# Output projection of a hybrid decoder block: sixteen plain products or one seven-product step

## The chip, the core and the metric

One core of one Trainium2 chip runs the whole program in one launch. Its engines work side by side, each through its own list of instructions in a fixed order, and wait for one another through semaphores: TensorE (PE in the profile) multiplies, VectorE (DVE), ScalarE (ACT) and GpSimd (POOL) work elementwise, and SyncE (SP) issues the transfers between DRAM and the on-chip memory SBUF. Products are written to PSUM, in eight banks of 128 x 512 float32. The metric is device time in microseconds (us), the median of the timed runs.

## The reference, cut to what matters

The program computes one decoder layer on 1024 tokens of width 1024, all in float32: a norm, an input projection, two groups of heads (retention and differential attention), the output projection with the residual, a second norm, and a SwiGLU feed-forward of width 2816.

```python
ret = ret * jax.nn.silu(rg)                       # [1, 1024, 512]
dif = (rms_norm(dif, diff_subln_g[l]) * (1.0 - LAMBDA_INIT)).reshape(B, S, DIFF_WIDTH)
mix = jnp.concatenate([ret, dif.astype(ret.dtype)], axis=-1)
x = x + jnp.einsum('bse,ed->bsd', mix, w_out[l]).astype(x.dtype)   # w_out 1024 x 1024
h2 = rms_norm(x, norm2_g[l])
ff = jax.nn.silu(jnp.einsum('bsd,df->bsf', h2, w_gate[l])) * jnp.einsum('bsd,df->bsf', h2, w_up[l])
x = x + jnp.einsum('bsf,fd->bsd', ff, w_down[l]).astype(x.dtype)
```

The change concerns the line with `w_out` and what stands next to it in time.

## The kernel before, in words

**Precision.** Every float32 operand of a product is split in two pages, `hi` (rounded to the matmul's fp32r type, a copy on ACT) and `lo` (the rest, a subtraction on DVE). One product of 128 x 128 by 128 x 512 is then three matmuls, hi·hi, hi·lo and lo·hi (`mm3`); I call that a triple.

**Stages.** Input projection of the attention heads and the attention itself run until about 225 us; the retention columns of the input projection follow, already as seven-product Strassen steps (`P1` to `P7`, one step for each half `p` of the retention heads), until about 420 us; then the output projection until about 541 us; then gate and up of the feed-forward, again as seven-product steps, until about 964 us; then the down projection, also in seven products.

**The output projection** (`o_proj`) takes sixteen pairs of a 128-token tile `t` and a column half `dh`, each with eight triples over the 1024 features: 16 x 8 x 3 = 384 matmuls. Its two operands are prepared beside it. `wo_prepare` loads a 128 x 512 page of `w_out`, scales and splits it (ACT and DVE). `mix_turn` loads the attention half of a token tile, transposes it and the retention half on PE, and splits both. When a pair is done, DVE adds the residual page of `x` from SBUF to the PSUM bank and SP stores the sum.

**What else runs in this stage.** The second four of the eight retention chunks of each half (`unit(p, t)`), a chain of small matmuls and DVE, ACT and POOL steps, are mixed in between the triples; `norm(t)` scales the finished rows and transposes them for the feed-forward; `f_sum` and `early_sums` form the sums of norm pages that the feed-forward's Strassen step needs as operands (`blk` names the seven operand pages). The first two feed-forward blocks' products (`first_product`) close this list.

**What sets the order.** Everything up to those first feed-forward products is registered with `add(engine, duration, ...)` in a list, and `Plan.times` works out an order for each engine: a list scheduling backwards from due times and forwards by assumed durations, tried with `SEEDS` small random shifts of the due times, the shortest kept. The order is then emitted as it stands, and the engines keep it. All those instructions are recorded by one helper, so the profile gives them all line L101, and groups are told apart by tiles: `h`, `pp`, `m` and `big` are PSUM banks, `whi`/`wlo` the split pages of the left operands, `sx` split pages of the right ones, `raw`, `pr`, `rowa` and `spare` plain pages, `wx`/`wy` the working pages of the retention chunks, `small` their row statistics. All plain transfers go through SP's one queue, in its order. The later feed-forward blocks are ordered by a hand-written pipeline (`class Strassen`), whose weight sums run on POOL (`sum<-rawp`, `sum<-wide`).

Of the kernel before, what the change touches and what calls it, by code (L numbers as in the profile page):

```python
# [72 lines left out]
def block_kernel(ctx: ExitStack, tc: tile.TileContext, x, norm1_g, w_in, ret_norm_g, dq_g, dk_g,  # L73
# [1057 lines left out]

    def wo_prepare(dh, k):
        key, page = wraw() if dh == 0 else wo1raw()
        dma(page, w_out[0, k * P:(k + 1) * P, dh * 512:(dh + 1) * 512], (), [key])
        hi, lo = wo_part(dh, k)
        kh, kl = wo_key(dh, k)
        scale = gout[:, min(k, 4):min(k, 4) + 1]
        after = [wo_after[dh][k // 4]]
        act_copy(hi, page, [key, "opened"], [kh], scale, after=after)
        stt(lo, page, scale, hi.bitcast(F32), ALU.mult, ALU.subtract, [key, kh], [kl], after=after)  # L1140
# [6 lines left out]
    xr_r = Ring(rawk)
    x2k = {}
    mT = {}

    DUE1 = {4: ("o", 0, 1), 5: ("o", 1, 1), 6: ("o", 1, 1), 7: ("o", 1, 1)}

    def mix_unit(t):
        if t < 4:
            key, page = prk[4 + t % 4]
            dma(page[:, 0:256], mixrd[t], [f"mixrd{t}"], [key])
        else:
            unit(0, t, marks[DUE1[t]])
        unit(1, t, marks[DUE1[t]] if t >= 4 else None)

    def mix_turn(t):
        key, page = px[t][1]
        dma(page, mixdd[t], [f"mixdd{t}"], [key])
        for q, (key, page) in enumerate((prk[4 + t % 4], px[t][1])):
            b = side_bank()

            def go(b=b, page=page):
                for j in range(4):
                    T.transpose(bank[b][:, j * P:(j + 1) * P], page[:, j * P:(j + 1) * P], ident)
            add("PE", 0.45, go, [key], [f"b{b}"])  # L1170
            n = 2 * (t % 2) + q
            hi, lo = slot[n]
            act_copy(hi, bank[b], [f"b{b}"], [f"wh{n}"], dur=0.48)
            tt(lo, bank[b], hi.bitcast(F32), ALU.subtract, [f"b{b}", f"wh{n}"], [f"wl{n}"])
# [417 lines left out]
```

## Time and profile before

| | value |
|---|---|
| median of three runs | 1179.95 us (1179.64, 1181.64, 1179.95) |
| the profiled execution | 1179.49 us |
| its span in the profile | 1177.7 us |
| PE busy | 1169.5 us, 99% of the span |
| DVE, ACT, POOL busy | 895.4, 604.5, 506.5 us (76%, 51%, 43%) |
| POOL between 419.95 and 545 us | 23.1 us, 44 instructions |

The span lies 1.8 us inside the execution's time. A share of busy time is a mean over stages that differ: POOL is at 43% over the whole program, but in the output projection it is nearly idle. Rows of a timeline give start, duration, engine, line, operation and tiles; rows of groups give busy time and the mean of one instruction after the bar, then the idle time ahead of the group's instructions with what ended most of it.

### The profile page before, as it was taken

How to read it: one execution, taken by the hardware profiler on the slowest of the kernel's cores; microseconds unless marked ns; L12 is line 12 of the kernel's file. 1: busy time of each engine (PE TensorE's matmuls, PEld its weight loads, DVE VectorE, ACT ScalarE, POOL GpSimd, SP SyncE). 2: the span in 40 equal slices, each digit the busy share in tenths (PEclk: the TensorE clock that was granted, in tenths of full speed). 3: DMA queues.
4: the chain of work that ended last, by engine and by line, in shares of the span. 5: the costliest groups of instructions: out<-in, count | busy, mean ns of one | idle time of the engine just before them, and what ended most of it. 6: DMA issues, size and time to landing. Idle time of an engine off the chain costs nothing.

```text
span 1177.7 us, 17427 instructions
## 1 busy us (share of the span) xinstructions
PE 1169.5 (99%) x5872; PEld 1004.7 (85%) x5872; DVE 895.4 (76%) x1561; ACT 604.5 (51%) x1332; POOL 506.5 (43%) x581
## 2 busy tenths in 40 slices
PE   9999999999999999999999999999999999999998
PEld 7999999988888888888888888888888888888887
DVE  6988888888779866758987756666665769698696
ACT  7767566666366745836444343434344334344442
POOL 4668786510012111301276654565456535263153
PEclk9999999999999999999999999999999999999999
DMA  7278776537644862322133423332323388933341
GB/s 213 69 173 150 136 115 117 162 124 235 223 126 148 266 201 90 95 88 90 58 131 117 134 76 98 111 119 90 99 99 116 106 293 265 354 101 90 98 138 67
DMA packets 118009, 164.29 MB, mean 139 GB/s; under 512 B 11936, under 2 KB 62240, under 8 KB 117792
## 3 DMA queue, kind: packets, MB, share of 16 engines
q1 hardware_dynamic: 110976, 152.62, 39.4%
q0 software_dynamic: 5760, 10.49, 6.5%
q8 instruction: 46, 0.75, 0.3%
q14 instruction: 43, 0.35, 0.1%
q10 hardware_dynamic: 1184, 0.07, 0.1%
HBM read 110.97 MB, written 54.26 MB: 140 GB/s over the span
## 4 chain that ended last, share of the span: by engine, by line
PE 93%; DVE 4%; ACT 2%; issue 1%; DMA 1%; SPq 0%; POOL 0%; DVEq 0%; ACTq 0%
PE h L101 39%; PE pp L101 31%; PE m L101 19%; PE big L101 4%; ACT pr L101 1%; DVE wx L101 1%; DVE wy L101 1%; DVE wlo L101 1%; DMA spare<-in_w_in_dram 1%; DVE pr L101 0%; DVE rowa L101 0%; DVE sx L101 0%; ACT wy L101 0%; DVE acc L101 0%; ACT whi L101 0%
## 5 line engine op out<-in xcount | busy, mean ns | idle before, releaser
L101 POOL TENSOR_TENSOR sum<-rawp 128x512 f32<-128x512 f32 x100 | 141.8, 1419 | 175.0 <-DVE wlo L101 144.9
L101 ACT CAST whi<-sum 128x512 fp32r<-128x512 f32 x155 | 96.4, 622 | 197.8 <-PE h L101 58.7
L101 DVE TENSOR_TENSOR wlo<-sum,whi 128x512 fp32r<-128x512 f32 x155 | 158.6, 1024 | 34.4 <-ACT whi L101 34.2
L101 PE MATMUL pp<-whi,act 128*128 128x384 f32 (+1 forms) x592 | 180.9, 359 | 0.2 <-DVE qkn L101 0.2
L101 POOL TENSOR_TENSOR sum<-wide 128x512 f32<-128x512 f32 x55 | 85.7, 1560 | 128.5 <-DVE wlo L101 101.8
L101 PEld LDWEIGHTS pp<-whi,act 128*128 128x128 f32 x592 | 109.4, 188 | 4.9 <-ACT q L101 0.6
L101 PE MATMUL h<-sx,whi 128*128 128x512 f32 x360 | 111.3, 390 | 0.0
L101 DVE TENSOR_TENSOR wlo<-wide,whi 128x512 fp32r<-128x512 f32 x99 | 77.5, 805 | 33.2 <-ACT whi L101 33.2
L101 ACT CAST whi<-wide 128x512 fp32r<-128x512 f32 x99 | 59.3, 621 | 84.2 <-PE m L101 43.3
L101 PE MATMUL pp<-wlo,act 128*128 128x384 f32 (+1 forms) x296 | 102.5, 346 | 0.0
L101 PEld LDWEIGHTS h<-sx,whi 128*128 128x128 f32 x360 | 67.2, 188 | 13.7
L101 DVE TENSOR_TENSOR wlo<-rawp,whi 128x512 fp32r<-128x512 f32 x44 | 48.6, 1105 | 38.6 <-ACT whi L101 37.7
L101 PE MATMUL h<-whi 128*128 128x512 f32 x196 | 76.7, 391 | 0.0
L101 DVE TENSOR_TENSOR c<-c,h 128x512 f32<-128x512 f32 x80 | 52.9, 681 | 31.3 <-PE h L101 31.3
L101 PE MATMUL h<-whi,wlo 128*128 128x512 f32 x196 | 76.3, 389 | 0.0
L101 PE MATMUL h<-wlo,whi 128*128 128x512 f32 x196 | 76.3, 389 | 0.0
L101 POOL TENSOR_TENSOR fsum<-c 128x512 f32<-128x512 f32 x50 | 70.7, 1426 | 8.1 <-DMA ffd<-fsum 8.1
L101 PE MATMUL h<-sx,wlo 128*128 128x512 f32 x180 | 70.1, 389 | 0.0
L101 POOL TENSOR_TENSOR stt<-stt,cs 128x1 f32<-128x1 f32 (+1 forms) x64 | 57.9, 906 | 3.7
L101 PEld LDWEIGHTS pp<-wlo,act 128*128 128x128 f32 x296 | 55.9, 189 | 1.9
L101 DVE CUSTOM_DVE_ANT_0 big<-big,zm 128x128 f32<-128x128 f32 (+7 forms) x64 | 47.7, 771 | 8.8 <-PE big L101 8.6
L101 PE MATMUL h<-b,whi 128*128 128x512 f32 x176 | 54.3, 390 | 0.0
(328 smaller groups left out, 3136.4 us busy)
## 6 DMA issues: line engine op xcount, KB each, us to landing
wide<-ffd SPq DMA_DIRECT2D x77, 256.0 KB, 2.7
ffd<-fsum SPq DMA_DIRECT2D x55, 256.0 KB, 2.0
rawp<-in_w_gate_dram SPq DMA_DIRECT2D x22, 512.0 KB, 3.5
rawp<-in_w_up_dram SPq DMA_DIRECT2D x22, 512.0 KB, 3.6
wide<-in_w_down_dram SPq DMA_DIRECT2D x44, 256.0 KB, 5.4
sumd<-act POOLq DMA_DIRECT2D x40, 256.0 KB, 4.2
rowa<-cd SPq DMA_DIRECT2D x32, 256.0 KB, 2.9
cd<-pr SPq DMA_DIRECT2D x24, 256.0 KB, 2.8
```

Of the source, the lines that this page charges most:

```text
L101: i = getattr(self.engine, op)(*(now(a) for a in args), **{k: now(a) for k, a in kw.items()})
```

## The change

The sixteen plain pairs are replaced by one Strassen step. Tokens, features and columns are halved; with A the mixed heads (columns: retention, attention) and B the output weights, seven products of a 512 x 512 block by a 512 x 512 block are formed, each in four token tiles of four triples: 7 x 4 x 4 x 3 = 336 matmuls.

- **Right operands** (`b_load`, `b_prepare`): 20 page loads in place of 16 (one quadrant's four pages are loaded twice, for products 3 and 6), each scaled in place by ACT. Five of the seven products need a sum or difference of two quadrants (20 pages, on POOL). All 28 operand pages are split, `hi` on ACT and `lo` on POOL. They go to two pages in turn (`HOME`).
- **Left operands** (`dif_turn`, `ret_turn`, `a_split`): the transposed tiles are copied to plain pages by ACT, DVE forms 20 sums and differences of quadrants, and 28 pages are split, `hi` on ACT, `lo` on DVE.
- **Results** (`o_product`, `o_add`): the residual pages are loaded ahead, and DVE adds each product to one or two of them, 40 additions in place of 16. Products 7 and 6 accumulate on the banks of 4 and 2 without clearing them.
- **Order**: products 4, 7, 1, 3, 5, then 2 and 6, which need the last retention chunks.
- **The feed-forward's first operands**: operand 3's sum and split and the nine `early_sums` go from DVE to POOL.
- **Homes**: new pages `kb` and `pg` (eight of 128 x 512 each) stand where `wo` and later operand pages stood; five of the seven `blk` pages get other homes; the cos/sin inputs of the later retention chunks come to pages of `rawp`. The planner tries 40 shifts, shifts only jobs from number 1700 on, and assumes 3.2 us of lag for a transfer in place of 2.8.

```diff
-                    j.shift = 0.0 if seed == 0 else 2.0 * (1 + seed % 3) * (...)
+                    j.shift = 0.0 if seed == 0 or j.n < SAME else 2.0 * (1 + seed % 3) * (...)
...
-    wo_block = [[sxt[0], sxt[2]], [None, lazy("wo")]]
...
+    HOME = {4: 0, 7: 1, 1: 0, 3: 1, 5: 0, 2: 1, 6: 0}
+    home_after = [[marks["P5", 3]], [marks["P7", 3]]]
...
+    def b_load(key, page, j, dh, k):
+        dma(page, w_out[0, (4 * j + k) * P:(4 * j + k + 1) * P, dh * 512:(dh + 1) * 512], (), [key])
+        act_copy(page, page, [key, "gout"], [key], gd if j else gout[:, k:k + 1])
+
+    TT_POOL = 1.5
+
+    def b_prepare(n, k):
+        (k0, b00), (k1, b11), (k2, b10) = kept_b[k], kept_b[4 + k], rowk[4 + k]
...
+        elif n == 1:
+            key, page = tmp_r()
+            tt(page, b00, b11, ALU.add, [k0, k1], [key], "POOL", TT_POOL)
...
+        hi, lo = b_part(n, k)
+        kh, kl = b_key(n, k)
+        act_copy(hi, page, [key], [kh], after=home_after[HOME[n]])
+        tt(lo, page, hi.bitcast(F32), ALU.subtract, [key, kh], [kl], "POOL", TT_POOL, after=home_after[HOME[n]])
...
+    def a_split(n, i, key, page, eng="DVE", dur=0.61):
+        at = A_SLOT[n] + i
+        hi, lo = slot[at]
+        act_copy(hi, page, [key], [f"wh{at}"])
+        tt(lo, page, hi.bitcast(F32), ALU.subtract, [key, f"wh{at}"], [f"wl{at}"], eng, dur)
...
+    def o_product(n, i, b, first=True):
...
+                for s_, (l, r) in enumerate(((ah, wh), (ah, wl), (al, wh))):
+                    T.matmul(bank[b], l[:, col], r, start=first and k == s_ == 0, stop=k == 3 and s_ == 2,
+                             skip_group_check=not first)
+            marks["o", n, i] = add("PE", MM3, go, [f"wh{at}", f"wl{at}"] + b_key(n, k), [f"b{b}"], main=True)
+
+    def o_add(t, dh, b, op=ALU.add):
+        key, page = px[t][dh]
+        tt(page, page, bank[b], op, [key, f"b{b}"], [key])
...
-    def o_proj(t, dh):
-        b = main_bank()
-        for k in range(KC):
...
-                mm3(bank[b], mh[:, col], ml[:, col], wh, wl, k == 0, k == KC - 1)
...
-        tt(page, bank[b], xr, ALU.add, [f"b{b}", xk], [key])
...
-    blk = [sxt[1], lazy("b1"), sxt[2], lazy("b3"), hT[1][1], sxt[0], lazy("wo")]
+    blk = [lazy("b0"), lazy("b1"), sxt[1], lazy("b3"), lazy("b4"), sxt[0], lazy("b6")]
...
-        eng, dur, e = ("DVE", 0.61, V)
+        eng, dur, e = ("POOL", TT_POOL, G) if b == 3 else ("DVE", 0.61, V)
...
-            tt(p0, p0, p1, ALU.add, [k0, k1], [k0])
+            tt(p0, p0, p1, ALU.add, [k0, k1], [k0], "POOL", TT_POOL)
...
-    for t, dh in PAIRS:
...
+    for i in range(4):
+        b = main_bank()
+        o_product(1, i, b)
+        o_add(i, 0, b)
+        o_add(4 + i, 1, b)
...
+    for n in (2, 6):
+        for k in range(4):
+            b_prepare(n, k)
+    for t in range(4, NT):
+        ret_turn(t)
...
+    for pair in ((0, 1), (2, 3)):
+        banks = [main_bank() for _ in pair]
+        for i, b in zip(pair, banks):
+            o_product(2, i, b)
...
+        for i, b in zip(pair, banks):
+            o_product(6, i, b, False)
...
+    for t in range(4, NT):
+        norm(t)
+        f_sum(4, t - 4)
```

How the instructions now stand is seen on three engines. On POOL, in the stretch of the output projection (`small` and `wy` belong to the retention chunks, `kb` to the kept quadrants of `w_out`, `sx` to the split operand pages), before:

```order
L101 TENSOR_TENSOR small<-small,cs 128x4
L101 TENSOR_TENSOR wy<-wy,cs 128x256 x2
L101 TENSOR_TENSOR small<-small,eps_199 128x4
L101 TENSOR_TENSOR small<-small,cs 128x4
L101 TENSOR_TENSOR wy<-wy,cs 128x256
```

and now:

```order
L101 TENSOR_TENSOR sum<-kb 128x512
L101 TENSOR_TENSOR sx<-sum,sx 128x512 x2
L101 TENSOR_TENSOR sum<-kb 128x512
L101 TENSOR_TENSOR small<-small,cs 128x4
L101 TENSOR_TENSOR sx<-sum,sx 128x512
L101 TENSOR_TENSOR small<-small,eps_199 128x4
L101 TENSOR_TENSOR sx<-pr,sx 128x512
L101 TENSOR_TENSOR small<-small,cs 128x4
L101 TENSOR_TENSOR sx<-raw,sx 128x512 x2
L101 TENSOR_TENSOR wy<-wy,cs 128x256 x2
L101 TENSOR_TENSOR pr<-pr,kb 128x512
L101 TENSOR_TENSOR sx<-pr,sx 128x512
```

Between the small steps of the chunks there now stand operations on whole 128 x 512 pages, the sums (`sum<-kb`, `pr<-pr,kb`) and the `lo` pages (`sx<-...,sx`).

On DVE, around the additions of the products (with buffer numbers), before, where `pr_2687<-pp_148,raw_114` is an addition of the residual:

```order
L101 TENSOR_TENSOR wy_3559<-m_151,wy_3559 64x2x64
L101 TENSOR_TENSOR wx_3558<-wx_3558 128x8x32
L101 TENSOR_TENSOR pr_2687<-pp_148,raw_114 128x512
L101 TENSOR_REDUCE small_2693<-wx_3558 128x4
L101 TENSOR_TENSOR wy_3559<-h_2908,cs_77 128x512
```

and now:

```order
L101 TENSOR_TENSOR rowa_117<-rowa_117,h_2903 128x512
L101 TENSOR_TENSOR pr_2686<-pr_2686,h_2903 128x512
L101 TENSOR_TENSOR wy_3558<-h_2905,cs_77 128x512
L101 TENSOR_TENSOR wlo_100<-pg_4262,whi_99 128x512
L101 TENSOR_TENSOR pg_4262<-pg_4262,spare_2631 128x512
L101 TENSOR_TENSOR rowa_118<-rowa_118,h_2904 128x512
L101 TENSOR_TENSOR pr_2687<-pr_2687,h_2904 128x512
L101 TENSOR_TENSOR wy_3558<-h_2905,cs_77 128x512
```

One finished bank (`h_2903`, `h_2904`) is now added to two pages, and between the additions stand a sum of quadrants (`pg<-pg,spare`) and a `lo` page (`wlo<-pg,whi`), whose two inputs both lie in SBUF.

On PE, where chunks and triples alternate (`cs` holds the identity for transposes), before:

```order
L101 MATMUL h_2906<-wo_4096,wlo_100 128x512
L101 MATMUL h_2908<-wx_3558,wy_3559 128x256 x2
L101 MATMUL h_2909<-wy_3559 128x128
L101 MATMUL h_2909<-wy_3559 128x64 x2
L101 MATMUL h_2909<-wy_3559 128x128
L101 MATMUL h_2909<-wy_3559 128x64 x2
L101 MATMUL m_150<-cs_77,wx_3558 128x128 x4
L101 MATMUL h_2907<-whi_105,whi_101 128x512
```

and now:

```order
L101 MATMUL h_2903<-sx_2995,wlo_98 128x512
L101 MATMUL pp_149<-cs_77,pg_4262 128x128 x4
L101 MATMUL h_2905<-wx_3557,wy_3558 128x256 x2
L101 MATMUL h_2903<-sx_2995,whi_97 128x512 x2
L101 MATMUL h_2903<-sx_2995,wlo_98 128x512
L101 MATMUL h_2904<-sx_2995,whi_99 128x512 x2
```

The triples' right operand now comes from an `sx` page that POOL has completed, and two token tiles (`h_2903`, `h_2904`) follow each other closely.

More of the change, by code (lines that the diff above doesn't have):

```diff
@@ L1092, in unit @@
         stay = p == 0 and t < 4
-        mk, m_ = onr if stay else prk[4 + t % 4]
+        mk, m_ = onr if stay else mixp[t]
         ob = m_ if stay else m_[:, 256 * p:256 * p + 256]
@@ L1132, in wo_prepare @@
[L1132 to L1140, printed above, removed]
-    for k in range(KC):
-        wo_prepare(0, k)
@@ L1144, in block_kernel, with open_kb @@
-    add("NONE", 0.0, lambda: open_act("wo", F32R), (), [f"R{i}" for i in range(8)] + ["opened"])
-    px = [[prk[t], rowk[(t + 4) % 8]] for t in range(NT)]
[L1147 to L1153, printed above, removed]
+    ap_keys = [f"K{i}" for i in range(8)]
+    def open_kb():
+        late["kb"] = late["sx"].tile([P, 8 * 512], F32, tag="sx", name="kb")
+    add("NONE", 0.0, open_kb, (), ap_keys, after=[marks["P3", 3]])
@@ new lines, in dif_turn, with ret_turn @@
+    def dif_turn(j, i):
+        key, page = stream()
+        dma(page, mixdd[4 * j + i], [f"mixdd{4 * j + i}"], [key])
+        bk, m = turned(key, page)
+        rk, raw = raw11[i] if j else raw01[i]
+        act_copy(raw, m, [bk], [rk], dur=0.48)
+        if j:
+            a_split(4, i, rk, raw)
+        else:
+            (ok, other), (tk, tmp) = raw11[i], tmp_r()
+            tt(tmp, raw, other, ALU.subtract, [rk, ok], [tk])
+            a_split(7, i, tk, tmp)
+    def ret_turn(t):
+        i = t % 4
+        bk, m = turned(*mixp[t])
+        (k0, a00), (k1, a11), (k2, a01) = raw00[i], raw11[i], raw01[i]
+        if t < 4:
+            act_copy(a00, m, [bk], [k0], dur=0.48)
+            tk, tmp = tmp_r()
+            tt(tmp, m, a11, ALU.add, [bk, k1], [tk])
+            a_split(1, i, tk, tmp)
+        else:
+            tt(a11, m, a11, ALU.add, [bk, k1], [k1])
+            tt(a00, a00, m, ALU.subtract, [bk, k0], [k0])
+            a_split(2, i, k1, a11)
+            a_split(6, i, k0, a00)
@@ L1156, in mix_unit @@
             dma(page[:, 0:256], mixrd[t], [f"mixrd{t}"], [key])
         else:
[L1158 to L1174, printed above, removed]
@@ new lines, in block_kernel @@
+    blk_after[6] = [add("NONE", 0.0, lambda: open_act("b6", F32R), (), [f"R{i}" for i in range(8)])]
+    for i in range(4):
+        norm(i)
+        f_sum(3, i)
+    for pair in ((0, 1), (2, 3)):
+        banks = [main_bank() for _ in pair]
+        for i, b in zip(pair, banks):
+            o_product(2, i, b)
+            o_add(4 + i, 0, b)
+            o_store(4 + i, 0)
+        for i, b in zip(pair, banks):
+            o_product(6, i, b, False)
+            o_add(4 + i, 1, b, ALU.subtract)
+            o_store(4 + i, 1)
@@ L1389, in block_kernel @@
+    for _ in range(2):
+        first_weights(*weights.pop(0), free_slots.pop(0))
+    for t in range(4, NT):
+        norm(t)
+        f_sum(4, t - 4)
+        if t < 7:
+            early_sums(t - 4)
+    blk_after.update({2: [marks["o", 2, 3]], 5: [marks["o", 6, 3]]})
     for b in (2, 5, 6):
```

195 lines of the change are left out of this document (127 added, 68 removed).

## The prediction

> **What bounds the kernel now.** I read the engine shares and the chain of waits on the page first, then PE's waits, then the stretches by window.
>
> ```profile
> PE 1169.5 (99%) x5872; PEld 1004.7 (85%) x5872; DVE 895.4 (76%) x1561; ACT 604.5 (51%) x1332; POOL 506.5 (43%) x581
> ...
> PE 93%; DVE 4%; ACT 2%; issue 1%; DMA 1%; SPq 0%; POOL 0%; DVEq 0%; ACTq 0%
> ```
>
> PE is busy for 99% of the span, and 93% of the chain that ended last is PE. Is that so in the stage that changes? PE's waits over the whole span, in us in total, count and longest:
>
> ```profile
> PE pp L101 <- DVE aT L101: 1.4, 1, 1.4
> PE big L101 <- ACT whi L101: 1.2, 1, 1.2
> PE m L101 <- DVE wx L101: 0.4, 1, 0.4
> PE pp L101 <- DVE b L101: 0.4, 1, 0.4
> ```
>
> Two waits are over half a microsecond, neither in the output projection (`aT` and `big` are pages of the attention). The windows give, for each stretch, its length and then the busy time of PE, PE's weight loads, DVE, ACT and POOL, each with its count:
>
> ```profile
> 419.95:545.00 125.05, 124.83 (x674) 106.33 (x673) 79.04 (x140) 70.44 (x188) 23.10 (x44) 1.00 0.34 109
> 510.00:562.00 52.00, 51.60 (x267) 43.77 (x266) 39.23 (x65) 29.20 (x60) 5.93 (x11) 1.00 0.25 82
> 600.00:900.00 300.00, 300.00 (x1325) 248.41 (x1324) 201.06 (x276) 121.71 (x210) 170.63 (x123) 1.00 0.32 107
> 975.00:1150.00 175.00, 175.00 (x774) 144.91 (x773) 147.21 (x173) 74.28 (x128) 71.54 (x46) 1.00 0.53 173
> ```
>
> In the output projection PE is busy 124.83 of 125.05 us at the full granted clock (1.00). So matmuls that are removed there shorten the program, as long as the others keep up: DVE uses 63% of this stretch, ACT 56%, POOL 18%. Between 510 and 562 us, at the norms, DVE is already at 75%.
>
> **What is removed from PE.** 384 matmuls become 336, 48 fewer, all of 128 x 512. One costs 300.00 / 1325 = 0.2264 us (the third window holds nothing else), so 48 x 0.2264 = **10.9 us**. The numbers of transposes stay, but the order has some ten more changes between the products and small matmuls. Their price:
>
> ```profile
> 444.89 0.62 PE L101 MATMUL h<-sx,whi 128*128 128x512 f32 x2
> 445.34 0.39 PE L101 MATMUL h<-sx,wlo 128*128 128x512 f32 x1
> 445.57 0.60 PE L101 MATMUL pp<-cs,pr 128*128 128x128 f32 x4
> 445.93 0.71 PE L101 MATMUL h<-sx,whi 128*128 128x512 f32 x2
> 446.48 0.39 PE L101 MATMUL h<-sx,wlo 128*128 128x512 f32 x1
> ```
>
> The pair of matmuls that opens a triple takes 445.34 - 444.89 = 0.45 us to the next one, and 446.48 - 445.93 = 0.55 behind a group of transposes: 0.1 us each, 1.1 us for ten or eleven. PE's own gain is 10.9 - 1.1 = **9.8 us**.
>
> **What is added to the other engines.** DVE gets 23 more instructions (before, 65 splits and sums; now 28 `lo` splits, 20 sums, 40 additions), ACT 56 more copies, POOL 65 operations of 128 x 512 (20 weight sums, 28 `lo` pages, 17 sums for the feed-forward). They aren't spread evenly: products 4 and 7 come early, and the eight late chunks, products 1, 3, 5, 2, 6 and the norms lie in one tight stretch. I count it in the changed order from product 7's last addition to the feed-forward's first products, and price each engine there.
>
> PE: 284 wide matmuls x 0.2264 = 64.3 us; chunks and transposes are the ones that took 125.05 - 384 x 0.2264 = 38.1 us in the first window; 24 of 384 columns and 24 of 128 from the feed-forward, about 3. Together some 105 us. DVE:
>
> ```profile
> 558.84 1.28 DVE L101 TENSOR_TENSOR sx<-pr,sx 128x512 fp32r<-128x512 f32 x2
> ...
> L101 DVE TENSOR_TENSOR wx<-wx 128x256 f32<-128x256 f32 x18 | 7.6, 439 | 1.2 <-PE pp L101 1.1
> L101 DVE SCALAR_TENSOR_TENSOR pr<-pr,small,rawp 128x512 f32<-128x512 f32 x8 | 6.0, 748 | 3.8 <-POOL small L101 3.8
> L101 DVE TENSOR_TENSOR wy<-m,wy 64x128 f32<-64x128 f32 x17 | 4.9, 286 | 0.7 <-PE m L101 0.4
> ```
>
> Two operations of 0.68 end within 1.28, so back to back one takes 0.60; the others lose the same 0.08. 60 with a PSUM input and 56 with two SBUF inputs x 0.60 = 69.6; 16 norm scalings x 0.67 = 10.7; 22 half pages x 0.36 = 7.9; 22 small x 0.21 = 4.6. That is 93 of 105 us: **12 us free**, where the first window leaves 46. ACT has 224 instructions there, and these rows:
>
> ```profile
> L101 ACT CAST whi<-raw 128x512 fp32r<-128x512 f32 x7 | 4.3, 618 | 3.1 <-DVE raw L101 3.1
> ...
> L101 ACT ACTIVATE pr<-pr,small 128x64 f32<-128x64 f32 x48 | 12.7, 341 | 1.6 <-POOL small L101 1.6
> ```
>
> The 48 short ones count 12.7 us, 0.26 each; with about half of the 224 short and half full pages (0.62, less about 0.03) ACT comes to some 96 us. POOL:
>
> ```profile
> L101 POOL TENSOR_TENSOR sum<-rawp 128x512 f32<-128x512 f32 x100 | 141.8, 1419 | 175.0 <-DVE wlo L101 144.9
> L101 POOL TENSOR_TENSOR sum<-wide 128x512 f32<-128x512 f32 x55 | 85.7, 1560 | 128.5 <-DVE wlo L101 101.8
> ...
> L101 POOL TENSOR_TENSOR small<-small,cs 128x4 f32<-128x4 f32 x12 | 12.4, 1033 | 0.9
> L101 POOL TENSOR_TENSOR wy<-wy,cs 128x256 f32<-128x256 f32 x9 | 6.4, 707 | 26.1 <-DVE wy L101 26.1
> ```
>
> 49 big operations x 1.42 = 69.6, 9 x 0.71 = 6.4, 12 row statistics x 1.03 = 12.4, and some 32 small ones of about 0.4 = 12.8: 101 us, of which the last nine `early_sums` (12.8) are wanted only later. So all three helpers are above 88% of PE's time in this stretch, and what decides is whether they also get in one another's way.
>
> **The disputed cost: DVE beside POOL.** Groups of DVE between 600 and 900 us, where POOL makes 123 operations:
>
> ```profile
> L101 DVE TENSOR_TENSOR wlo<-sum,whi 128x512 fp32r<-128x512 f32 x80 | 62.7, 784 | 24.9 <-ACT whi L101 24.9
> L101 DVE TENSOR_TENSOR c<-c,h 128x512 f32<-128x512 f32 x65 | 43.0, 681 | 25.4 <-PE h L101 25.4
> L101 DVE TENSOR_TENSOR wlo<-rawp,whi 128x512 fp32r<-128x512 f32 x33 | 36.5, 1105 | 33.9 <-ACT whi L101 33.1
> L101 DVE TENSOR_TENSOR c<-c 128x512 f32<-128x512 f32 x32 | 26.7, 834 | 0.3
> ```
>
> One operand in PSUM (`c<-c,h`): 681 ns always. Both in SBUF: 784 to 1105. And between 975 and 1150 us, groups and one moment:
>
> ```profile
> L101 DVE TENSOR_TENSOR wlo<-wide,whi 128x512 fp32r<-128x512 f32 x86 | 65.6, 788 | 27.8 <-ACT whi L101 27.8
> L101 DVE TENSOR_TENSOR wlo<-sum,whi 128x512 fp32r<-128x512 f32 x43 | 62.1, 1445 | 0.0
> ...
> 1036.99 0.68 DVE L101 TENSOR_TENSOR wlo<-wide,whi 128x512 fp32r<-128x512 f32 x1
> 1037.15 1.68 POOL L101 TENSOR_TENSOR sum<-wide 128x512 f32<-128x512 f32 x1 [0.63 <-DVE wlo L101]
> 1037.59 1.78 DVE L101 TENSOR_TENSOR wlo<-sum,whi 128x512 fp32r<-128x512 f32 x1
> ```
>
> The DVE operation that starts while POOL's runs ends at 39.37, 0.54 after POOL's end at 38.83: it has stood still for 1.10 us. So each operation of POOL can block DVE for 0 to 1.10 us, only where DVE's next one reads SBUF twice. What does it average? Between 600 and 900 us the excess over 681 is 80 x 0.103 + 33 x 0.424 + 32 x 0.153 = 27.1 us for 123 operations, **0.22 us** each, with 145 such DVE operations in 300 us (0.48 per us). Between 975 and 1150 it is 86 x 0.107 + 43 x 0.764 = 42.1 for 46, **0.91**; there one `lo` page follows each of POOL's sums in a fixed beat, and the other kind alone makes 9.2 / 46 = 0.20. The new stretch has no such beat, but (56 + 16 + 22) / 105 = 0.90 such operations per us: I scale 0.22 by 0.90 / 0.48 and take **0.40**. It has 49 big operations, nine of which can run late, and nine of half size: about 44, so 44 x 0.40 = 17.6 us more for DVE against 12 free: some **6 us** in which PE waits for a `lo` page or for an addition to free its bank. The bounds are 44 x 0.22 = 9.7 (no stall) and 44 x 0.91 = 40 (28 of stall).
>
> Less matters elsewhere. ACT's copies and the `x` loads lie beside PE. The loads of `w_out` are 20 for 16.
>
> ```profile
> rowa<-cd SPq DMA_DIRECT2D x32, 256.0 KB, 2.9
> wide<-ffd SPq DMA_DIRECT2D x77, 256.0 KB, 2.7
> ```
>
> A load of 256 KB lands in 2.9 us and is issued ahead; if the cover is gone each one costs up to that. The new order of shifts also changes where the feed-forward releases its pages: the first page for the down projection comes free 49 matmuls ahead of its use in place of 73. 49 x 0.2264 = 11.1 us against 2.7 + 0.62 + 1.11 = 4.4 of load, copy and split: still covered, so nothing.
>
> **The sum.** Against the profiled execution of 1179.49: -10.9 + 1.1 + 6 = -3.8, 1175.7. That run lies 0.46 under the median of 1179.95; by the median it is 1176.1. I forecast **1176 us**.
>
> **Rivals.**
>
> *All hidden.* The planner's order leaves enough slack, and blocked time stays under 12 us (up to 0.27 per POOL operation; 600 to 900 us shows 0.22). Then the whole 9.8 us arrive: 1179.95 - 9.8 = **1170**. Against it stand three helpers near 90%.
>
> *DVE blocked in earnest.* It ends on the other side. If DVE, never idle in this stretch, meets nearly each POOL operation with an SBUF pair waiting, it loses about the middle between 0.40 and the 1.10 us seen at 1037.59: 44 x 0.75 = 33, less 12 free = 21 of stall, 1179.95 - 9.8 + 21 = **1191**. The place is products 1 to 6, the point from which it costs more than it gains (12 + 9.8) / 44 = 0.50 us per operation. For it speaks the row of 1445 ns; against it the 784 ns of the same tiles from 600 to 900 us, and that over half of DVE's operations in the stretch are not affected by POOL. The Trainium skill, "SBUF — State Buffer", section "Who interferes with whom", has a rule that speaks for this rival: a DVE instruction with two SBUF inputs and a GpSimd instruction that reads SBUF exclude each other, and the second one blocks for the whole of the first, not for a share. The row of 1.78 us agrees. By that rule alone, with a random start inside POOL's 1.42 us the mean wait of one that is hit would be an estimated 0.7 us, as in this rival; by the 600 to 900 us rows it is 0.22 per operation.
>
> *POOL itself is the bound.* `lo` pages of the weights now hang on POOL, each behind an ACT copy, in an order kept as it stands. At the 1.56 us of `sum<-wide` its 101 us become 49 x 0.14 = 6.9 more, 108 against PE's 105; with an estimated 0.3 us of idle time at each of 28 `lo` pages (8.4, half a copy's 0.62 each), PE loses 11: 1179.95 - 9.8 + 11 = **1181**. For it: product 1's operand pages can be split only when product 4 has finished with the same page, and are needed next but one. Against it: POOL's work before the stretch starts earlier.
>
> *Late pages.* SP's transfers wait in order, and a `w_out` page waits for POOL to free its buffer; behind it stand the `x`, `cd` and `w_gate` loads. Three such turns at 2.9 us plus a copy (0.62) cost 10.6: about **1181** too, less if they overlap.
>
> **Chances.** The forecast with 2 to 8 us of stall (1172 to 1178) 0.38; all hidden 0.16; DVE blocked 0.20; POOL the bound 0.16; late pages 0.10. For 8 times in 10 I take 1169 to 1189: the lower end is the full gain and 1 us, the upper one holds the lighter half of the blocked case (0.70 per operation) and leaves the rest out. A measurement of this kernel tells changes over 0.2% (2.4 us). Faster by more than that, under 1177.6: most of the forecast's share (0.33), all hidden (0.16): 0.49. Within it: the rest of the forecast (0.05) and half of the two 1181 cases (0.13): 0.18. Slower: 0.33.
>
> **What would show it.** PE's records fall from 5872 by about 48; POOL's busy time in the stage rises from 23 to some 115 us; DVE's groups with two SBUF tiles (`wlo<-pg,whi`, `pg<-pg,spare`, `wlo<-sum,whi`) have means of 850 to 1050 ns there while additions stay near 681; PE's waits now name DVE in this stage, with 4 to 8 us in total. Waits on POOL's `sx` would show the third rival, waits on transfers the fourth. A PE without new waits, or with over 12 us of them, makes the forecast wrong; so would a loss in the feed-forward, whose instructions I hold to be unchanged.

## The result and the profile after

| | before | changed |
|---|---|---|
| median | 1179.87 us (1179.64 to 1181.64, 4 runs) | 1201.57 us (1198.81 to 1203.37, 4 runs) |
| ratio | | 1.0179, 95% interval 1.0167 to 1.0192 |
| profiled span | 1177.7 us | 1200.5 us |

The changed kernel is slower by 21.7 us, where 4 us of gain were forecast and 1169 to 1189 us allowed. The page of the changed kernel, engines and chain of waits:

```profile
PE 1171.8 (98%) x5824; PEld 1002.5 (84%) x5824; DVE 940.0 (78%) x1584; ACT 636.9 (53%) x1388; POOL 607.5 (51%) x646
...
PE 88%; DVE 8%; issue 2%; DMA 1%; POOL 0%; ACT 0%; SPq 0%; DVEq 0%
```

PE has the 48 matmuls fewer (5824 for 5872), yet it is busy 2 us longer, and idle 1200.5 - 1171.8 = 28.7 us where it was 8.2. DVE's share of the chain has doubled. The longest of PE's waits in the changed kernel:

```profile
PE pp L101 <- DVE b L101: 10.1, 6, 3.0
PE m L101 <- DVE wx L101: 3.8, 2, 2.8
PE pp L101 <- DVE wlo L101: 2.3, 1, 2.3
PE pp L101 <- DVE rowa L101: 1.9, 2, 1.1
...
PE h L101 <- DVE wy L101: 1.4, 1, 1.4
...
PE h L101 <- POOL wy L101: 0.4, 1, 0.4
```

Between 395 and 585 us the waits that name DVE come to 21 us, the one on POOL to 0.4; none names a transfer. Where do they lie? Stretches of the changed kernel (columns as in the prediction's windows):

```profile
400.00:440.00 40.00, 37.22 (x199) 31.45 (x197) 34.13 (x49) 25.59 (x64) 24.85 (x21) 0.96 0.75 245
440.00:480.00 40.00, 34.49 (x174) 27.86 (x174) 37.57 (x52) 28.47 (x68) 28.99 (x25) 0.96 0.25 83
480.00:536.00 56.00, 53.39 (x304) 45.49 (x302) 50.02 (x90) 43.91 (x122) 36.40 (x42) 1.00 0.30 99
536.00:592.00 56.00, 44.95 (x223) 36.61 (x222) 55.03 (x69) 36.87 (x76) 34.30 (x31) 0.94 0.16 52
...
600.00:1200.50 600.50, 596.40 (x2632) 493.50 (x2630) 431.66 (x550) 240.96 (x414) 302.11 (x208) 1.00 0.40 134
```

and of the kernel before, from the same place in the feed-forward (2633 matmuls from the end) on:

```profile
577.00:1177.70 600.70, 596.65 (x2633) 493.71 (x2631) 435.04 (x552) 241.54 (x416) 303.29 (x209) 1.00 0.40 133
```

The feed-forward behind that place takes 600.5 and 600.7 us: nothing is lost there. The loss lies between 400 and 592 us, mostly in two heaps: 8.3 us of idle PE from 400 to 480 (products 4, 7 and 1 and the preparation of their weight pages) and 11.1 us from 536 to 592 (the norms and the feed-forward's first operands); from 480 to 536 us it is 2.6. In the second heap DVE is busy 55.03 of 56 us. What does it do? DVE's groups between 400 and 585 us:

```profile
L101 DVE TENSOR_TENSOR wx<-rawp,cs 128x512 f32<-128x512 f32 x18 | 18.0, 1019 | 0.1
L101 DVE TENSOR_TENSOR wlo<-spare,whi 128x512 fp32r<-128x512 f32 x16 | 15.8, 1005 | 0.3 <-ACT whi L101 0.3
L101 DVE TENSOR_TENSOR wx<-wx 128x256 f32<-128x256 f32 x20 | 13.6, 688 | 0.1
L101 DVE TENSOR_TENSOR pr<-pr,h 128x512 f32<-128x512 f32 x15 | 10.2, 680 | 0.6 <-PE h L101 0.5
...
L101 DVE TENSOR_TENSOR b<-sum,b 128x512 fp32r<-128x512 f32 x4 | 5.9, 1493 | 0.0
```

The additions from PSUM (`pr<-pr,h`) take 680 ns as ever. Nearly all groups with two inputs in SBUF are longer: `wx<-wx` 688 for 439, `wlo<-spare,whi` 1005 for some 683, `b<-sum,b` 1493. Over all such groups of this view the excess is about 36.5 us. Beside them POOL made 58 operations of 128 x 512 and ten half ones: 0.58 us each, with two halves counted as one. One moment, DVE and POOL in order of time:

```profile
548.33 0.68 DVE L101 TENSOR_TENSOR wlo<-rawp,whi 128x512 fp32r<-128x512 f32 x1
548.77 1.39 POOL L101 TENSOR_TENSOR sum<-rowa,pr 128x512 f32<-128x512 f32 x1
548.93 1.78 DVE L101 TENSOR_TENSOR wlo<-raw,whi 128x512 fp32r<-128x512 f32 x1
...
550.64 0.74 DVE L101 SCALAR_TENSOR_TENSOR rowa<-rowa,small,rawp 128x512 f32<-128x512 f32 x1
550.73 1.78 POOL L101 TENSOR_TENSOR b<-sum,b 128x512 fp32r<-128x512 f32 x1
551.30 0.68 DVE L101 TENSOR_TENSOR b<-pp,b 128x512 fp32r<-128x512 f32 x1
551.90 1.16 DVE L101 SCALAR_TENSOR_TENSOR pr<-pr,small,rawp 128x512 f32<-128x512 f32 x1
```

The second `wlo` starts 0.16 us into a POOL operation and lasts 1.10 us too long; at 551.30 an operation with a PSUM input runs beside POOL's without loss. POOL's operation at 550.73, which starts 0.09 us into a scaling of DVE with two SBUF inputs, takes 1.78 us where the prediction's rows give 1.42: it looks as if POOL were held up in turn.

### The profile page after: what moved, and what is told of

Its sections match the earlier page's. It is cut to its first block, busy times and chain, and to the rows that moved or that the text cites. A ratio compares the mean times of both kernels' runs of the same rounds, so it can differ in the third digit from the quotient of the medians.

```text
span 1200.5 us, 17466 instructions
## 1 busy us (share of the span) xinstructions
PE 1171.8 (98%) x5824; PEld 1002.5 (84%) x5824; DVE 940.0 (78%) x1584; ACT 636.9 (53%) x1388; POOL 607.5 (51%) x646
## 4 chain that ended last, share of the span: by engine, by line
PE 88%; DVE 8%; issue 2%; DMA 1%; POOL 0%; ACT 0%; SPq 0%; DVEq 0%
PE h L101 36%; PE pp L101 30%; PE m L101 18%; PE big L101 4%; DVE wx L101 2%; DVE wlo L101 2%; DVE pr L101 1%; DVE rowa L101 1%; DVE wy L101 1%; DVE sum L101 1%; DVE b L101 0%; DVE pg L101 0%; DMA rawp<-in_w_gate_dram 0%; DVE raw L101 0%; POOL sx L101 0%
## 5 line engine op out<-in xcount | busy, mean ns | idle before, releaser
L101 DVE TENSOR_TENSOR wlo<-sum,whi 128x512 fp32r<-128x512 f32 x163 | 164.1, 1007 | 33.3 <-ACT whi L101 33.1
L101 PE MATMUL h<-b,whi 128*128 128x512 f32 x432 | 133.4, 390 | 0.0
L101 PEld LDWEIGHTS h<-b,whi 128*128 128x128 f32 x432 | 80.8, 188 | 16.6
L101 PE MATMUL h<-b,wlo 128*128 128x512 f32 x216 | 84.1, 389 | 0.0
L101 PE MATMUL pp<-b,whi 128*128 128x512 f32 (+2 forms) x240 | 72.6, 384 | 5.7 <-DVE b L101 5.7
L101 PEld LDWEIGHTS h<-sx,whi 128*128 128x128 f32 x336 | 61.4, 188 | 11.9 <-ACT whi L101 0.4
L101 PE MATMUL m<-b,whi 128*128 128x512 f32 x224 | 70.1, 394 | 0.0
L101 PE MATMUL h<-whi 128*128 128x512 f32 x176 | 68.5, 389 | 0.0
L101 PE MATMUL h<-wlo,whi 128*128 128x512 f32 x176 | 68.5, 389 | 0.0
L101 PE MATMUL h<-whi,wlo 128*128 128x512 f32 x176 | 68.5, 389 | 0.0
```

The costliest lines, as they stand in the source:

```text
L101: i = getattr(self.engine, op)(*(now(a) for a in args), **{k: now(a) for k, a in kw.items()})
```

## Experiments

Four theories are told apart. **A**: DVE's own time is the bound, its work plus its standstill beside POOL. **B**: POOL is slow, so its pages come late. **C**: DVE just has too many instructions. **D**, formed on the way, when A had missed: the reader of SBUF that DVE's second input and POOL use in turn is the bound, and DVE's other work does not count. The edits are to the changed kernel unless another is named; "same order" means that the planner's durations and dependencies were kept, so that every instruction stands where it stood.

**POOL busy, but not reading.** Same order; the diff is of the first run, the second has one fill in place of three:

```diff
+        if eng == "POOL" and dur == 1.5:
+            return add(eng, dur, lambda: fill(to), r, w, **kw)
...
+    def fill(to):
+        for _ in range(3):
+            G.memset(to.bitcast(F32), 0.0)
```

> The changed kernel's order, every instruction in its place, but each of POOL's 65 operations on 128 x 512 is replaced by three fills of the same page with zero (about 0.5 us each, together as long as the operation): POOL is as busy as before and reads nothing from SBUF. The weights' lo pages and the sums formed on POOL are left out of the computation. Theory A (VectorE is the bound between 440 and 590 us, since its operations with two SBUF inputs stand still while POOL reads: 36.6 us of excess over the unhindered durations in that stage): the excess goes, these operations fall to 0.68 us, PE's waits vanish, 1168 to 1174 us. Theory B (POOL's own length makes its pages late): stays at 1195 to 1203. Theory C (VectorE simply has 23 instructions too many): 1188 to 1196, VectorE still saturated.

> As the run with three fills, but with one fill of some 0.5 us for each of the 65 operations, so POOL is short as well as not reading. The same parts are left out of the computation. Theory A: no different from three fills, 1168 to 1174. Theory B: only here does the time fall, to 1170, while three fills stay near 1200. Theory C: 1188 to 1196 in both.

Three fills: **1172.67 us**, 0.9928 of before (0.9904 to 0.9951). One fill: **1168.82 us**, 0.9894 (0.9866 to 0.9922). DVE's groups between 400 and 570 us with three fills, and POOL's from 380:

```profile
L101 DVE TENSOR_TENSOR wx<-rawp,cs 128x512 f32<-128x512 f32 x18 | 12.4, 705 | 0.1
L101 DVE TENSOR_TENSOR wlo<-spare,whi 128x512 fp32r<-128x512 f32 x15 | 10.1, 683 | 1.5 <-ACT whi L101 1.5
L101 DVE TENSOR_TENSOR b<-sum,b 128x512 fp32r<-128x512 f32 x5 | 3.4, 684 | 0.2 <-ACT b L101 0.2
...
L101 POOL MEMSET sx<- 128x512 f32 x84 | 43.5, 526 | 5.6 <-PE h L101 2.3
```

POOL is as busy as before, three fills of 0.526 us for each operation, and DVE's means are back at 0.68. So 28.9 of the 32.8 us between the changed kernel and the run with one fill go with POOL's reading; C falls, and B keeps 3.9 us, the difference of the two runs. PE's own gain is there in full: 1180.23 - 1168.82 = 11.4 us, 9 to 16 by the interval.

**The work of POOL back on DVE**, all of it, or only the 17 operations for the feed-forward; both with a new order. The first edit stands for all weight sums and splits and is made in the first run alone, the other two in both:

```diff
-            tt(page, b10, b00, ALU.subtract, [k2, k0], [key], "POOL", TT_POOL)
+            tt(page, b10, b00, ALU.subtract, [k2, k0], [key], "DVE", 0.61)
...
-        eng, dur, e = ("POOL", TT_POOL, G) if b == 3 else ("DVE", 0.61, V)
+        eng, dur, e = ("DVE", 0.61, V) if b == 3 else ("DVE", 0.61, V)
...
-            tt(p0, p0, p1, ALU.add, [k0, k1], [k0], "POOL", TT_POOL)
+            tt(p0, p0, p1, ALU.add, [k0, k1], [k0])
```

> The Strassen step with nothing on POOL: all 65 operations on VectorE at 0.61 in the planner, which works out a new order. Theory A: VectorE gets 49 x 0.60 = 29 us more in the tight stretch and loses 36.6 us of standstill, so it still binds and the time is a little under the changed kernel's: 1189 to 1198. Theory B: POOL was the bound, so 1170 to 1180. Theory C: 29 us more on an engine that is already the bound, 1215 to 1230.

> Only the 17 operations for the feed-forward's operands (operand 3's sums and splits, the nine early sums) go back to VectorE, as before the change; the weight pages stay on POOL; new order. Theory A: 17 x 0.60 = 10 us more for VectorE, and 17 x 0.65 = 11 us less of standstill: 1196 to 1203, no difference. Theory B: POOL's end is shorter by 24 us, 1180 to 1190. Theory C: 1208 to 1213.

All on DVE: **1184.69 us**, 1.0034 (1.0022 to 1.0045), between B's range and A's and in neither. The 17 alone: **1194.58 us**, 1.0113 (1.0084 to 1.0141), 7 us under the changed kernel where A forecast none, and above B's 1180 to 1190. As far as two new orders can show it, both say that an operation on POOL costs DVE more than the 0.6 us of doing it itself. But DVE alone does not carry the step either; the run with everything on DVE:

```profile
480.00:500.00 20.00, 19.96 (x112) 16.72 (x111) 19.81 (x40) 15.88 (x44) 7.18 (x11) 1.00 0.20 72
...
520.00:540.00 20.00, 18.07 (x100) 13.87 (x99) 20.00 (x33) 16.62 (x40) 6.31 (x14) 1.00 0.22 81
540.00:560.00 20.00, 16.61 (x85) 13.45 (x84) 20.00 (x34) 12.06 (x22) 0.00 (x0) 0.93 0.24 79
```

Until 500 us PE loses next to nothing; then DVE is full for 20 of 20 us and PE waits.

**Parts of the change in the kernel before**: only the 17 operations for the feed-forward to POOL (the edit is made at the sum, at its `lo` page and at the early sums), and only the planner's numbers (with the shifts from job `SAME` on and 3.2 us of lag for a transfer).

```diff
-        eng, dur, e = ("DVE", 0.61, V)
+        eng, dur, e = ("POOL", 1.5, G) if b == 3 else ("DVE", 0.61, V)
```

```diff
-    GAP, GAP_PE, AHEAD, SEEDS = 0.12, 0.4, 8.0, 32
+    GAP, GAP_PE, AHEAD, SEEDS, SAME = 0.12, 0.4, 8.0, 40, 1700
```

> One part of the change alone, put into the kernel before: its sixteen plain pairs stay, only operand 3's sums and splits and the nine early sums go to POOL (17 operations of 128 x 512), with a new order. Theory A (an operation that POOL takes over saves VectorE 0.6 us and blocks it for as much, when VectorE is the engine without slack): VectorE is at 75% between 510 and 562 us and full only behind 540, so 17 x (0.58 - 0.60) is about nothing: 1177 to 1184 us, no difference. If the hand-over were a gain, 1172 to 1177 could not come either, since PE is at 99%; if POOL's slowness hurt by itself, the sums at 1.42 us would come late: 1184 to 1192.

> The kernel before with nothing but the planner's three numbers of the change (40 shifts, shifts from job 1700 on, 3.2 us of lag for a transfer), so a new order of the same instructions. Theory A: PE stays the bound, 1178 to 1183 us. If the planner's numbers and the luck of an order made the loss, 1190 or more.

With the 17 on POOL: **1186.93 us**, 1.0050 (1.0033 to 1.0066), above what A allowed and in the range given for POOL's sums coming late; yet PE's longest new wait, 2.3 us, names DVE's `b`, and none names POOL. The new order alone: **1180.51 us**, 0.9993 (0.9982 to 1.0004), nothing. A window of the first of the two:

```profile
540.00:560.00 20.00, 16.20 (x80) 13.48 (x78) 20.00 (x26) 14.62 (x29) 10.62 (x7) 0.91 0.29 93
```

PE loses 3.8 us there, DVE is full, and the granted clock falls. So this part of the change, with the order that goes with it, costs 6.7 us by itself, with no Strassen step at all.

**POOL reading one stream, not two.** Same order; each of the 65 is a copy:

```diff
+        if eng == "POOL" and dur == 1.5:
+            return add(eng, dur, lambda: G.tensor_copy(to, b), r, w, **kw)
```

> The changed kernel's order, but each of POOL's 65 operations is a copy of one of its two inputs to the same page, so that POOL reads one stream from SBUF where it read two; the weights' lo pages and the sums formed on POOL are left out of the computation. I know no duration of such a copy from these traces; between the fill's 0.53 and the sum's 1.42 us. If any reading by POOL blocks VectorE's operations with two SBUF inputs, the excess is as long as the copies are: at 0.8 us each 58 x 0.33 = 19 us in place of 36.6, 1175 to 1184 us. If only POOL's second input collides, as with the fills: 1169 to 1173, means of 0.68.

**1175.55 us**, 0.9947 (0.9931 to 0.9964), at the lower edge of the range for any reading. The copy's own length and the DVE group that still suffers most:

```profile
L101 POOL CAST sx<-sx 128x512 fp32r<-128x512 f32 x28 | 20.4, 738 | 19.8 <-ACT sx L101 19.6
...
L101 DVE TENSOR_TENSOR wx<-rawp,cs 128x512 f32<-128x512 f32 x18 | 14.5, 822 | 0.1
```

A copy lasts 738 ns, half the sum's 1.42 us, and DVE is still blocked at times: this group takes 822 ns, for 705 with fills and 1019 in the changed kernel, and over all groups with two SBUF inputs the excess is some 10 us in place of 36.5, far less than half. Whether that is the shorter time or the single stream, this run does not tell.

**Leaving out operations of one kind.** Same order: the second addition of products 1, 3 and 5 (12 of DVE's, from PSUM); POOL's nine early sums; the eight `lo` pages of the norms (DVE, from PSUM); operand 4's four sums and four `lo` pages (DVE, both inputs in SBUF). For the last two, ACT fills the `lo` page by a copy.

```diff
+        if skip:
+            add("DVE", 0.61, lambda: None, [key, f"b{b}"], [key])
+            return
...
-        o_add(4 + i, 1, b)
+        o_add(4 + i, 1, b, skip=True)
...
```

```diff
-            tt(p0, p0, p1, ALU.add, [k0, k1], [k0], "POOL", TT_POOL)
+            add("POOL", TT_POOL, lambda: None, [k0, k1], [k0])
```

```diff
-                tt(lo, bank[b], hi.bitcast(F32), ALU.subtract, bks + [f"k{q}{t % 4}h"], [f"k{q}{t % 4}l"])
+                add("DVE", 0.61, lambda lo=lo, hi=hi: A.copy(lo, hi.bitcast(F32)), bks + ...
```

```diff
+        add(eng, dur, (lambda: None) if b == 4 else (lambda: e.tensor_tensor(out=opened["sum"][n], ...
...
+        add(eng, dur, (lambda: A.copy(lo, hi.bitcast(F32))) if b == 4 else ...
```

> The changed kernel's order with the second addition of products 1, 3 and 5 left out (12 of VectorE's 40 additions; these contributions are missing in the sums). POOL does all its work. Theory A: VectorE is the bound, so 12 x 0.60 = 7.2 us less on it are 7 to 9 us less in all: 1191 to 1196 us. If POOL or the order of the transfers set the time: no change, 1199 to 1203.

> The changed kernel's order with the nine early sums left out on POOL (the feed-forward's operands 2, 5 and 6 lack their second term); POOL's other 56 operations stay. It asks whether a POOL operation costs what it blocks: between 540 and 576 us the changed kernel's VectorE stands still 12.8 us for 15 of POOL's big operations, 0.85 each, where the mean of the whole stage is 0.58. Theory A by the local price: 9 x 0.85 = 7.7 us, and some of the lowered clock behind the stall, so 1191 to 1195 us. By the mean of the stage: 9 x 0.58 = 5.2, 1195 to 1198. If VectorE's number of instructions alone binds: no change, 1199 to 1203, as with the twelve additions.

> The changed kernel's order with VectorE's eight lo pages of the norms left out (their one input lies in PSUM, so POOL cannot block them); a copy on ScalarE fills the page, so the feed-forward's operands 0 and 1 have a wrong lo part. Theory A (VectorE's time is the bound, 0.60 each): 4.8 us less, and some of the lowered clock, 1193 to 1197 us. Theory D (the reader that VectorE and POOL share is the bound, these operations don't use it): 0 to 2 us less, 1198 to 1202.

> The same order and stage with eight operations of the other kind left out, operand 4's four sums and four lo pages (both inputs in SBUF); a copy on ScalarE fills the lo page, so operand 4 is wrong. Four of the eight stand at 1493 ns and four at 1161 in the changed kernel. Theory A: 8 x 0.60 of work and up to 8 x 0.65 of standstill, 5 to 10 us, 1191 to 1197. Theory D: no less than 8 x 0.60 of the shared reader, 5 to 10 us too. So the pair of runs decides: A has both fall by 5 or more, D only this one.

| left out | kind | time | ratio to before | gain over the changed kernel |
|---|---|---|---|---|
| 12 additions | DVE, PSUM input | 1199.79 | 1.0158 (1.0141 to 1.0175) | 1.8 us, 0.15 each |
| 8 `lo` pages of norms | DVE, PSUM input | 1198.29 | 1.0153 (1.0135 to 1.0170) | 3.3 us, 0.4 each |
| 8 sums and `lo` pages | DVE, two SBUF inputs | 1192.89 | 1.0107 (1.0092 to 1.0122) | 8.7 us, 1.1 each |
| 9 early sums | POOL | 1189.13 | 1.0078 (1.0062 to 1.0094) | 12.4 us, 1.4 each |

The gains hold a share of lowered clock. The mean granted clock is 0.994 in the changed kernel, 0.998 without the early sums and 0.997 without operand 4's pages, so an estimated 5 of the 12.4 us and 3.5 of the 8.7 are clock; what is left is some 0.8 us for an operation of POOL and 0.65 for one of DVE with two SBUF inputs. Without the early sums the time lies below A's range too (1191 to 1195). A, by which twelve additions were worth 7 to 9 us, missed; those twelve stood between 460 and 523 us, nine of them behind 478, where little was lost. The other three stood at the same place, the norms. There, with the clock's share, an operation of POOL is worth its whole length, one of DVE with two SBUF inputs more than its own, one with a PSUM input little. How that comes about is seen in DVE's groups from 540 to 576 us, in the changed kernel:

```profile
L101 DVE TENSOR_TENSOR b<-sum,b 128x512 fp32r<-128x512 f32 x4 | 5.9, 1493 | 0.0
L101 DVE SCALAR_TENSOR_TENSOR rowa<-rowa,small,rawp 128x512 f32<-128x512 f32 x5 | 4.8, 969 | 0.0
L101 DVE TENSOR_TENSOR sum<-pr,rowa 128x512 f32<-128x512 f32 x4 | 4.6, 1161 | 0.0
...
L101 DVE SCALAR_TENSOR_TENSOR pr<-pr,small,rawp 128x512 f32<-128x512 f32 x4 | 4.2, 1050 | 0.0
L101 DVE TENSOR_TENSOR b<-pp,b 128x512 fp32r<-128x512 f32 x6 | 4.1, 678 | 0.0
```

and with the eight `lo` pages from PSUM (`b<-pp,b`) left out:

```profile
L101 DVE SCALAR_TENSOR_TENSOR pr<-pr,small,rawp 128x512 f32<-128x512 f32 x4 | 6.0, 1506 | 0.0
L101 DVE TENSOR_TENSOR b<-sum,b 128x512 fp32r<-128x512 f32 x4 | 5.9, 1495 | 0.0
L101 DVE TENSOR_TENSOR sum<-pr,rowa 128x512 f32<-128x512 f32 x4 | 5.7, 1433 | 0.0
...
L101 DVE SCALAR_TENSOR_TENSOR rowa<-rowa,small,rawp 128x512 f32<-128x512 f32 x4 | 3.0, 740 | 0.0
```

Most of the time that the left-out operations set free went into more standstill of the others: 1050 became 1506 and 1161 became 1433, while the scaling of `rowa` fell from 969 to 740. Over all groups of the two views the standstill rose from 12.8 to some 15.8 us, 3 us for the 3.6 of work (six operations) that is gone. That is what D says. The changed kernel's count from 540 to 576 us fits it: POOL's 15 big operations x 1.42 are 21.3 us, DVE's 30 with two SBUF inputs x 0.60 are 18.0, together 39 us in 36, so the pair is full; DVE's own 39 operations alone would be 23.4. The sum is 3 us more than the stretch holds, so a part of each operation must still run beside the other, and the full lengths count somewhat too much.

The intervals of the two runs without operations from PSUM touch that of the changed kernel, so their gains may be nothing; those of the other two do not. In both runs without `lo` pages ACT makes a copy for each of them, eight and four; in the first, PE's waits that name ACT's `b` pages come to 2.2 us, so D's advantage over A is shown less surely than the cost of POOL's reading.

**Divisions of the work that might have won.** On POOL only the weights of products 5, 2 and 6 (the diff), or of 2 and 6, the rest on DVE:

```diff
+    def on(n):
+        return ("POOL", TT_POOL) if n in (5, 2, 6) else ("DVE", 0.61)
...
-            tt(page, b10, b00, ALU.subtract, [k2, k0], [key], "POOL", TT_POOL)
+            tt(page, b10, b00, ALU.subtract, [k2, k0], [key], *on(n))
```

> A division of the work by where POOL blocked little: between 480 and 536 us the changed kernel lost 0.24 us per POOL operation, elsewhere 0.5 to 0.85. So the weights of products 5, 2 and 6 (16 operations) stay on POOL, those of 4, 7, 1 and 3 and the 17 operations for the feed-forward go to VectorE, with a new order. Theory A (price by place): the losses are those of the run without POOL until 480 us (0.2 us), those of the changed kernel until 536 (2.6), and 2 to 6 behind it: 1173 to 1181 us. If POOL's operations cost 0.58 wherever they stand: as the run with everything on VectorE, 1183 to 1187.

> As the run before it, with only the weights of products 2 and 6 on POOL (12 operations), those of product 5 on VectorE too. Theory A: four operations more on VectorE, 2.4 us, less 4 x 0.24: 0 to 2 us over the run before it, 1174 to 1183 us. If POOL's operations cost the same everywhere: 1183 to 1187.

**1190.46 us**, 1.0080 (1.0067 to 1.0094), and **1184.45 us**, 1.0038 (1.0025 to 1.0051). Both missed A's range; the first lies above the other range as well, the second lies within it (1183 to 1187). The planner, whose durations know nothing of blocking, put ten of POOL's 16 operations of the first run at 460 to 500 us, where DVE was full. In that run, one window, and DVE's and POOL's groups from 440 to 520 and 540 us:

```profile
460.00:480.00 20.00, 16.98 (x88) 14.20 (x86) 19.84 (x28) 12.17 (x37) 14.39 (x12) 0.91 0.21 65
...
L101 DVE TENSOR_TENSOR pg<-pg,wy 128x256 f32<-128x256 f32 x8 | 8.1, 1016 | 0.0
...
L101 POOL TENSOR_TENSOR sx<-kb,sx 128x512 fp32r<-128x512 f32 x8 | 12.6, 1600 | 0.0
```

A half page, 540 ns in the changed kernel, took 1016. The price of 0.24 us per POOL operation from 480 to 536 us did not carry over to another order.

**The norms' scaling on ACT**, nothing on POOL: for all halves of the rows, or only for the half that is not split.

```diff
-            add("DVE", 0.67, lambda page=page, q=q: V.scalar_tensor_tensor(
+            act_copy(page, page, [key, sk], [key], ss[:, 0:1])
...
+                for j in range(4):
+                    A.activation(page[:, j * P:(j + 1) * P], bank[b][:, j * P:(j + 1) * P], AF.Copy,
+                                 scale=g2col[:, 4 * q + j:4 * q + j + 1])
```

> The Strassen step with nothing on POOL (as the run with everything on VectorE, 1184.7 us) and, beside it, VectorE relieved at the norms: ScalarE scales each finished row by its statistic, and the gain g is applied by ScalarE when it copies the transposed page out of PSUM, in four pieces with g as a scale per partition; VectorE's 16 scalings of 0.67 to 0.75 us go, ScalarE gets some 21 us more, of 59 us that it had free between 380 and 600 us. Nothing is left out. Theory A: VectorE's load is the bound, and 16 x 0.67 = 10.7 us of it goes from the part where PE waits (540 to 600 us, 8.5 us of idle time and lowered clock there): 1175 to 1180 us, no slower than the kernel before and perhaps faster. If ScalarE's longer way (scale, transpose, four pieces, copy) is what PE waits for next: 1182 to 1188.

> As the run with the norms on ScalarE, nothing on POOL, but only one of the two halves of each row (the one that is only copied) goes to ScalarE, which with all of them was full (20.0 of 20 us from 520 to 540). VectorE loses 8 x 0.67 = 5.4 us, ScalarE gets 8 x (0.84 + 4 x 0.5 - 0.6) = 18. Theory A: between the run with everything on VectorE (1184.7) and the full gain, 1176 to 1182 us, ScalarE at about 85%. If the longer way costs more than it frees: 1184 to 1190.

**1189.74 us**, 1.0075 (1.0061 to 1.0089), and **1186.04 us**, 1.0048 (1.0032 to 1.0064): no gain over the 1184.69 with everything on DVE, and neither in A's range; the second lies in the range for a longer way that costs more than it frees, the first above its 1182 to 1188. In the first one the wait only changed its name; a window of it, PE's longest wait, and ACT's scaling:

```profile
520.00:540.00 20.00, 14.44 (x65) 11.05 (x64) 8.96 (x15) 20.00 (x63) 4.32 (x12) 0.83 0.17 64
...
PE pp L101 <- ACT rowa L101: 4.6, 2, 2.5
...
L101 ACT ACTIVATE rowa<-rowa,small 128x512 f32<-128x512 f32 x8 | 6.7, 834 | 0.0
```

DVE is at 8.96 of 20 us, ACT at 20.00. No version that computes everything beat the kernel before; the best of the Strassen step stand 4 us above it.

## Why the prediction was wrong, point by point

- **PE's gain was right.** 9.8 us were forecast, 10.9 without the switches; the run with one fill, whose PE does all the changed kernel's matmuls in its order, is 11.4 us under the kernel before.
- **What was missed, in the two profiles.** Forecast was a span 3.8 us shorter, measured one 22.8 us longer, 26.6 between them. PE's idle time grew by 20.5 us where 6 were forecast (14.5 more), and its busy time by 2.3 where it was to fall by 9.8 (12.1 more). The new waits on DVE, 21 us, pass the 12 beyond which the prediction called itself wrong.
- **The mechanism was named, and its size failed.** The step that failed is "I scale 0.22 by 0.90 / 0.48 and take 0.40" for what one POOL operation costs DVE. Measured: 0.58 on the mean of the stage; at the norms 0.85 (12.8 us for 15 operations). In the stretch that the prediction counted, from product 7's last addition to the feed-forward's first products (451.5 to 574 us of the changed kernel), POOL made 39 big operations and seven half ones, and DVE stood still some 25 us for the 17.6 forecast, 0.60 each. The density was scaled by 1.9, the price rose by 2.7: the fuller DVE was, the dearer an operation of POOL, 0.24 us where DVE was busy 50 of 56 us and 0.85 where it was busy 36 of 36.
- **The margin was too wide.** Of these 25 us, 17.6 reached PE (busy 104.89 of 122.5 us), where 6 were forecast: about 8 were covered, not the 12 that were "free". Another 3.4 us of idle PE lie between 400 and 451.5 us, where the prediction had put nothing, since "products 4 and 7 come early". By D, "12 us free" also added up the wrong thing: work from PSUM does not compete with POOL, so what had to fit into 105 us was POOL's reading and DVE's operations with two SBUF inputs. From the same counts: 49 x 1.42 + 9 x 0.71 = 76 us and 72 x 0.60 + 22 x 0.36 = 51 us, together 127 us, 22 too many. The sum would have been 1179.95 - 9.8 + 22 = 1192; this is worked out after the result, and no run tests it as a forecast.
- **A term was missing: the lowered clock.** The mean granted clock is 0.994 over the span, 0.999 in the run with one fill: about 6 us of the 12.1 by which PE was busy longer than forecast. Of the 32.8 us between these two runs, 21.1 are idle PE (28.7 less 7.6) and about 6 the clock; the remaining 6 are counted as busy PE, and the rows do not divide them further.
- **The rival that came true is the second, blocked DVE.** Its point of decision, 0.50 us per operation, was exceeded. Its stall of 21 us is near the 20.5 by which PE's idle time grew, in part by luck: it took 0.75 us per operation and 12 us of margin, where 0.60 and about 8 were measured, and the 3.4 us ahead of the stretch make up the rest. Its time, 1191, fell short by PE's longer busy time, the lowered clock and what is not divided. It had a chance of 0.20, too little for three engines over 88%. The Trainium skill, "SBUF — State Buffer", section "Who interferes with whom", limits its rule to a GpSimd instruction that reads SBUF, not one that only writes it; the run with three fills agrees (683 ns beside a POOL that only writes). The prediction named this rule and weighed it less than the average of 600 to 900 us.
- **POOL itself the bound**, the third rival, is worth 3.9 us (three fills against one), not 11. **Late pages** did not come as a wait of PE: none names a transfer, and the feed-forward from 600 us on is as long as before, the down projection's later release included.
- **"All hidden"** is what the fills show, 1169 to 1173, and what no division of the real work reached.

## What to carry to other kernels

Before work is moved from VectorE to GpSimd, add up two sums for the tightest stretch: VectorE's whole time, and GpSimd's reading time plus VectorE's operations with both inputs in SBUF; by these runs the larger one comes near to what binds, and in the second a GpSimd operation counts for up to its full length (1.42 us for 0.60 saved; leaving nine out gained 1.4 each, some 0.8 without the clock's share). A mean price per operation taken from a stage with slack was too low here for the stage without, 0.22 for 0.60. A planner that gives an engine fixed durations cannot see this: here it placed such work where VectorE was full.

## What the runs showed of the hardware that was not expected

PE's granted clock fell after short gaps. In the changed kernel, windows of 4 us around three of them:

```profile
408.00:412.00 4.00, 1.22 (x8) 0.77 (x7) 3.94 (x7) 2.10 (x5) 4.00 (x4) 1.00 0.83 286
412.00:416.00 4.00, 4.00 (x20) 3.47 (x18) 3.97 (x4) 2.12 (x7) 3.04 (x4) 0.63 0.08 29
...
456.00:460.00 4.00, 1.57 (x8) 0.84 (x7) 4.00 (x4) 2.91 (x9) 3.66 (x3) 1.00 0.84 258
460.00:464.00 4.00, 4.00 (x15) 3.17 (x15) 3.51 (x7) 2.79 (x6) 2.09 (x2) 0.60 0.35 116
...
572.00:576.00 4.00, 1.06 (x5) 1.07 (x6) 4.00 (x5) 2.14 (x4) 1.73 (x2) 0.68 0.43 131
576.00:580.00 4.00, 4.00 (x14) 3.43 (x14) 4.00 (x8) 3.73 (x9) 0.00 (x0) 0.50 0.02 4
```

One wait of 2.8 us (on `DVE wx`) was followed by 4 us at 0.63, one of 2.3 (on `DVE wlo`) by 4 us at 0.60, and 2.9 us of idle time by 4 us at 0.50; gaps of 0.5 to 1.8 us between 544 and 564 us and one of 2.2 at 566 left the clock at 1.00. So a stall of about 3 us cost 4.3 to 5: 2.8 and 4 x 0.37, 2.9 and 4 x 0.50. The Trainium skill, "TensorE: Matmul & The Clock Gate", "Part 1: The HAM clock gate", gives half rate after an idle window of about 3.4 us; the 0.50 agrees, and here gaps somewhat shorter than that were enough.
